# Gate products at eviction, short products queued later, and a pace of modulation loads by layer, in a four-layer RWKV-7 / GLA / SSD kernel

## The chip, the core and the metric

One of the eight cores of a Trainium2 chip runs the whole program; the seven others are idle. The metric is the device time of one execution in microseconds (us), the median of several runs. TensorE (PE) multiplies, VectorE (DVE) and ScalarE (ACT) work elementwise, SyncE (SP) and GpSimd (POOL) issue the transfers here.

## The reference, cut to what matters

A stream x of 256 tokens and 2048 features goes through four layers: RWKV-7, GLA, SSD, RWKV-7. Each layer adds to x:

```
mod = silu(c) @ ada_w[i] + ada_b[i]                  # 2048 x 6144 weights for a single vector c
shift, scale, gate = split(mod, 3)
h   = rms_norm(x, norm_g[i]) * (1 + scale) + shift
x   = x + gate * mixer(h)                            # then a final rms_norm
GLA, per head (4; keys 256, values 512):
  o = causal(q k^T with decays) v + q state          # chunks of 64
  y = rms_norm(o) * head_g * silu(g);  mixer = y @ w_out          # q, k, v, g: h @ w_in
SSD, per group (8; 8 heads of 64, state 128):
  x, B, C = silu(conv4(h @ w_in)), z = h @ w_in;  dt = softplus(...)
  y = causal(C B^T * decay) (x dt) + C state + d x   # chunks of 128
  y = rms_norm(y * silu(z), per group) * norm_g;  mixer = y @ w_out
```

## The kernel before

**Projections.** `jobs` computes blocks of 256 output columns. For each 128 x 1024 piece of weights (512 KB) it issues a load on SP into one of six `raw` buffers (`load_w`), lets ACT round it to H (L338) and DVE subtract it to L (L340), three buffers each, and issues 24 matmuls (L393: four k-tiles, two column tiles, three products of the split). Then it calls `tick`. "A tick" is such a piece below. The result lies in an `acc` bank of PSUM (two of them) and an `evac` function takes it out.

**Modulation.** The vector-matrix product with `ada_w` isn't done on PE: `ada_third` loads 128 x 1024 pieces (512 KB each, into the same six `raw` buffers, on the same SP queue) and DVE multiplies and accumulates them (L304; the first of 16 by ACT). Layer 0's shift and scale come first; then there are 320 pieces, 32 for each third (shift, scale, gate) of a layer. `tick` advances a generator over them: after tick n it has advanced `interp(n, PACE)` pieces, at most two more at a time, and not at all while `hold` is set (from the last output block of a layer until the next layer's first block is done). `ada_need` pulls at once, whatever is missing, when a layer needs a third: shift and scale at its start, the gate at its first output block. Pieces that `ada_need` pulls aren't counted by the pace.

**Layers in ticks.** Layer 0: 8 ticks of v (24 earlier pieces of v don't tick), 32 of k, 32 of r, 32 of g, and the output projection in three parts of 16, 16 and 8 ticks (`o4`, `o3`, `o1` below), together 144. Layer 1 (GLA): 4 for the decays, 8 for each head's v, 4 for q, 4 for k, 8 for g, and 16 for the output projection of each pair of heads, together 132, up to tick 276. Layer 2 (SSD): 2 for dt, then for each of eight groups 4 for B and C, 8 for x, 8 for z, and 16 for the output projection of each pair of groups, together 226, up to tick 502. Layer 3: 168.

**The order of the work.** A planner orders each engine's instructions when the program is built: it takes, by a model of the chip, the instruction that comes earliest in the program among those that it holds ready. The program's order is thus a priority and not the order of issue; at run time each engine follows the planned order. In a GLA head the program's order is v, q, k, then the scores (L1167), transposes of k (L1183), values (L1190 to L1200), the head's rms (L1204 to L1209), transposes of O (L1212) with an ACT copy to `oT`, then the output projection of the previous pair (`due()`), then g, whose `evg` (L1217 to L1224) computes silu(g), multiplies by `oT` and splits the result into `ys`, the input of the output projection. In an SSD group: B and C with their convolution, scores and decays (L1311 to L1341), x with its convolution, transposes of x (L1348), state (L1356), values (L1366 to L1372), `due()`, z with `evz` (L1375 to L1388), the group's rms (L1393, `inv_rms`) and `ys` (L1397). The last pair's output projection follows the last z or g at once; it goes through eight blocks, each over all k-tiles of the pair, two ticks each. After the last layer's last block `norm` sums squares (L454, L471), takes an inverse root by twelve small DVE operations (L1041 to L1049), and spreads it with a matmul (L483) before the next layer's input can be made.

Of the kernel before, what the change touches and what calls it, by code (L numbers as in the profile page):

```python
# [129 lines left out]
class Kern:  # L130
    def __init__(self, ctx, tc, A, out, layers=(0, 1, 2, 3), final=True):
# [15 lines left out]
        self.hold = False  # L147
        self.par = self.const.tile([P, NPAR], F32, name="par")
# [267 lines left out]
    def outproj(self, wv, k0, ys, i, norm=None):  # L416
# [10 lines left out]
        for n0 in range(0, D, cols):  # L427
            def evac(j, ps, n0=n0):
# [10 lines left out]
            self.hold = bool(norm) and n0 == D - cols  # L439
            self.proj(wv, n0, cols, ys, evac, k0=k0)  # L440
# [33 lines left out]
    def inv_rms(self, ps, mul, eps, bank):  # L474

        nc = self.nc
        rs = self.rsqrt_tiny(ps[:, 0:2], mul, eps, self.nrm)
        dg = self.nrm.tile([P, T], F32, name="xm", bufs=2)
        for c in range(2):
            nc.vector.tensor_scalar(out=dg[:, c * P:(c + 1) * P], in0=self.c("ident"), scalar1=rs[:, c:c + 1],  # L480
                                    scalar2=None, op0=ALU.mult)
        ps = bank()
# [627 lines left out]
    def paired(self, n, part, wout, i):  # L1110

        ys, k0, due = [], 0, []
        for g in range(n):
            ys += part(g, lambda: due and due.pop()())
            if g % 2:
                due.append(lambda ys=ys, k0=k0, norm=self.b1 if g == n - 1 else None:
                           self.outproj(wout, k0, ys, i, norm))
                ys, k0 = [], k0 + 8
        due.pop()()

    def gla_head(self, h, hs, win, bc, due, vt):
# [33 lines left out]
        self.proj(win, 1024 + 256 * h, 256, hs, evk)  # L1155


        HS = (slice(0, 64), slice(64, 128))
        ps = self.b1()
        for s in range(2):  # L1160
            for bi in range(2):
                i = slice((2 * s + bi) * C, (2 * s + bi + 1) * C)
                for kk in range(2):
                    for bj in range(2):
                        j = slice((2 * s + bj) * C, (2 * s + bj + 1) * C)
                        l, r = (ke, qe) if bi == bj else (kn, qs)
# [12 lines left out]

        kt = gu.tile([P, 2, P], F32, name="kt")  # L1180
        ps = self.b1()
        for kk in range(2):
            nc.tensor.transpose(ps[:, kk * P:(kk + 1) * P], kn[:, kk, 0:P], self.c("ident"))  # L1183
        nc.scalar.copy(out=kt.rearrange("p a c -> p (a c)"), in_=ps[:, 0:T])

        O = gu.tile([P, 2, 512], F32, name="O", bufs=1)
        S = gu.tile([P, 2, 512], F32, name="S")
        for s in range(2):
            ps = self.b1()
            nc.tensor.matmul(ps, sT[:, s, :], vt[:, s, :], start=True, stop=s == 0)  # L1190
            if s:
                for kk in range(2):
                    nc.tensor.matmul(ps, qs[:, kk, P:], S[:, kk, :], start=False, stop=kk == 1)
            nc.scalar.copy(out=O[:, s, :], in_=ps)
            if not s:
                for kk in range(2):
                    ps = self.b1()
                    nc.tensor.matmul(ps, kt[:, kk, :], vt[:, 0, :], start=True, stop=True)
                    nc.scalar.copy(out=S[:, kk, :], in_=ps)

        var = gu.tile([P, 2], F32, name="var")
        for tt in range(2):
            sq = gu.tile([P, 512], F32, name="osq", bufs=1)
            nc.scalar.activation(sq, O[:, tt, :], AF.Square)  # L1204
            nc.vector.tensor_reduce(out=var[:, tt:tt + 1], in_=sq, op=ALU.add, axis=mybir.AxisListType.X)
# [266 lines left out]
```

## Time and profile before

| | |
|---|---|
| median of 3 runs | 2873.01 us (2872.56 to 2883.22) |
| profiled execution | 2887.0 us, of which the span is 2885.0 |
| PE busy | 2686.2 us, 93% |
| DVE busy | 2212.4 us, 77% |
| ACT busy | 1392.8 us, 48% |
| granted TensorE clock, mean | 0.952 |
| moved by DMA | 673.68 MB, 234 GB/s over the span |

The busy shares are means over stages with different limits. In the tables of stretches below each engine's busy time stands with its number of instructions in brackets; PEclk is the mean granted clock of TensorE in the stretch as a share of 2.4 GHz. For layer 0 the stretches shown are k, r, g, o3, and o1 with the boundary to GLA. A stretch begins and ends at the first projection matmul (L393) of a stage, found by counting these matmuls in order of time (24 to a tick).

### The profile page before, as it was taken

How to read it: one execution, taken by the hardware profiler on the slowest of the kernel's cores; microseconds unless marked ns; L12 is line 12 of the kernel's file. 1: busy time of each engine (PE TensorE's matmuls, PEld its weight loads, DVE VectorE, ACT ScalarE, POOL GpSimd, SP SyncE). 2: the span in 40 equal slices, each digit the busy share in tenths (PEclk: the TensorE clock that was granted, in tenths of full speed). 3: DMA queues.
4: the chain of work that ended last, by engine and by line, in shares of the span. 5: the costliest groups of instructions: out<-in, count | busy, mean ns of one | idle time of the engine just before them, and what ended most of it. 6: DMA issues, size and time to landing. Idle time of an engine off the chain costs nothing.

```text
span 2885.0 us, 64064 instructions
## 1 busy us (share of the span) xinstructions
PE 2686.2 (93%) x26098; PEld 2505.1 (87%) x26098; DVE 2212.4 (77%) x3918; ACT 1392.8 (48%) x2315; POOL 154.6 (5%) x298
## 2 busy tenths in 40 slices
PE   6899999999987899988998999999889999999997
PEld 4789889887877899987988999999879988988887
DVE  5778777877788888877898788887668897666666
ACT  3475655433335454434544454554457756453333
POOL 0011110101000000000000000000000111010100
PEclk8899999999998999999999999999989999999999
DMA  9866557977677888976784767776557665585543
GB/s 348 308 231 190 176 161 261 347 266 278 207 261 244 293 285 291 324 268 197 277 294 161 242 219 228 224 226 216 167 171 236 230 208 190 178 297 194 207 132 108
DMA packets 239126, 673.68 MB, mean 234 GB/s; under 512 B 72272, under 2 KB 78416, under 8 KB 235760
## 3 DMA queue, kind: packets, MB, share of 16 engines
q1 hardware_dynamic: 217904, 580.84, 60.2%
q0 software_dynamic: 20928, 88.75, 8.5%
q8 instruction: 205, 3.36, 0.5%
q14 instruction: 89, 0.73, 0.1%
HBM read 620.66 MB, written 48.82 MB: 232 GB/s over the span
## 4 chain that ended last, share of the span: by engine, by line
PE 66%; DVE 8%; DMA 8%; issue 3%; ACT 2%; SPq 1%; POOL 0%; DVEq 0%; ACTq 0%; POOLq 0%
PE acc L393 53%; DMA raw<-in_ada_w 3%; DVE L L340 2%; PE g L785 2%; DVE adaacc L304 1%; ACT H L338 1%; PE b L897 1%; DMA raw<-in_gla_w_in 1%; DMA dx<-bd 1%; DMA raw<-in_rwkv_w_in 1%; PE b L866 1%; DMA raw<-in_rwkv_w_out 1%; PE b L873 1%; DMA sp<-yd 1%; PE b L1030 1%
## 5 line engine op out<-in xcount | busy, mean ns | idle before, releaser
L393 PE MATMUL acc<-xs,H 128*128 128x256 f32 x8480 | 1634.4, 291 | 36.5 <-ACT H L338 8.1
L393 PEld LDWEIGHTS acc<-xs,H 128*128 128x128 f32 x8480 | 1362.8, 196 | 69.3 <-ACT H L338 11.4
L393 PE MATMUL acc<-xs,L 128*128 128x256 f32 x4240 | 1230.6, 291 | 17.1 <-DVE L L340 16.2
L338 ACT CAST H<-raw 128x1024 fp32r<-128x1024 f32 (+1 forms) x706 | 718.0, 1018 | 854.9 <-PE acc L393 634.3
L340 DVE TENSOR_TENSOR L<-raw,H 128x1024 fp32r<-128x1024 f32 (+1 forms) x706 | 833.7, 1183 | 248.9 <-ACT H L338 234.0
L393 PEld LDWEIGHTS acc<-xs,L 128*128 128x128 f32 x4240 | 830.8, 196 | 31.1 <-DVE L L340 21.5
L304 DVE SCALAR_TENSOR_TENSOR adaacc<-raw,cact,adaacc 128x1024 f32<-128x1024 f32 x300 | 384.0, 1280 | 132.6 <-DMA raw<-in_ada_w 130.2
L393 PE MATMUL acc<-ys,H 128*128 128x256 f32 x1536 | 293.3, 291 | 12.2 <-DVE ys L409 4.9
L393 PEld LDWEIGHTS acc<-ys,H 128*128 128x128 f32 x1536 | 245.9, 195 | 22.0 <-issue 6.6
L393 PE MATMUL acc<-ys,L 128*128 128x256 f32 x768 | 222.1, 290 | 0.4 <-DVE L L340 0.4
L393 PEld LDWEIGHTS acc<-ys,L 128*128 128x128 f32 x768 | 149.6, 195 | 4.6 <-issue 3.6
L551 ACT ACTIVATE hn<-x,mod,omu 128x256 f32<-128x256 f32 x192 | 113.4, 599 | 1.5 <-DVE x L542 1.2
L431 DVE SCALAR_TENSOR_TENSOR x<-acc,mod,x 128x256 f32<-128x256 f32 x192 | 83.6, 477 | 35.7 <-PE acc L393 35.3
L393 PE MATMUL acc<-H,xs 128*128 128x256 f32 x512 | 97.1, 290 | 1.6 <-ACT vt L1078 1.6
L554 DVE SCALAR_TENSOR_TENSOR xm<-x,par,hn 128x256 f32<-128x256 f32 x192 | 88.6, 476 | 1.4 <-ACT hn L551 0.3
L393 PEld LDWEIGHTS acc<-H,xs 128*128 128x128 f32 x512 | 82.4, 197 | 3.1 <-ACT vt L1078 1.8
L393 PE MATMUL acc<-L,xs 128*128 128x256 f32 x256 | 73.8, 289 | 0.0
L785 PE MATMUL g<-abkp 64*128 64x128 f32 x768 | 65.8, 293 | 4.0 <-DVE G L823 2.7
L408 ACT CAST xs<-xm 128x256 fp32r<-128x256 f32 x128 | 50.9, 400 | 35.4 <-DVE xm L554 33.0
L785 PEld LDWEIGHTS g<-abkp 64*128 64x128 f32 x768 | 52.2, 190 | 15.8 <-issue 8.8
L1284 DVE SCALAR_TENSOR_TENSOR cva<-cvp,hcw,cva 128x256 f32<-128x256 f32 x144 | 64.9, 476 | 0.0
L278 DVE SCALAR_TENSOR_TENSOR adaacc<-raw,cact,adaacc 128x512 f32<-128x512 f32 x56 | 41.9, 748 | 27.5 <-DMA raw<-in_ada_w 23.0
(358 smaller groups left out, 3063.0 us busy)
## 6 DMA issues: line engine op xcount, KB each, us to landing
raw<-in_ada_w SPq DMA_DIRECT2D x384, 512.0 KB, 4.8
raw<-in_rwkv_w_in SPq DMA_DIRECT2D x256, 512.0 KB, 4.7
raw<-in_ssd_w_in SPq DMA_DIRECT2D x128, 512.0 KB, 4.4
raw<-in_gla_w_in SPq DMA_DIRECT2D x96, 512.0 KB, 5.2
raw<-in_ssd_w_out SPq DMA_DIRECT2D x64, 512.0 KB, 4.2
raw<-in_rwkv_w_out SPq DMA_DIRECT2D x48, 512.0 KB, 4.2
abkp<-kd POOLq DMA_DIRECT2D x16, 1024.0 KB, 7.3
raw<-in_gla_w_out SPq DMA_DIRECT2D x32, 512.0 KB, 4.9
```

The costliest lines, as they stand in the source:

```text
L278: nc.vector.scalar_tensor_tensor(out=acc, in0=raw[:, u, :], scalar=self.cact[:, k:k + 1], in1=acc, op0=ALU.mult, op1=ALU.add)
L304: nc.vector.scalar_tensor_tensor(out=acc, in0=raw, scalar=self.cact[:, k:k + 1], in1=acc, op0=ALU.mult, op1=ALU.add)
L338: nc.scalar.copy(out=hi, in_=raw[:, a:a + n])
L340: nc.vector.tensor_tensor(out=lo, in0=raw[:, a:a + n], in1=hi, op=ALU.subtract)
L393: self.nc.tensor.matmul(ps, lhs, rhs, start=first and part == 0 and w is hi, stop=last and w is lo)
L408: nc.scalar.copy(out=t[:, 0, :], in_=src)
L431: nc.vector.scalar_tensor_tensor(out=self.x[:, t, 1:], in0=ps[:, u, :], scalar=gate[:, t:t + 1], in1=self.x[:, t, 1:], op0=ALU.mult, op1=A ...
L551: nc.scalar.activation(t1, x[:, k, 1:], AF.Identity, scale=self.omu[:, col:col + 1], bias=self.mods[(i, 0)][:, k:k + 1])
L554: done[k] = nc.vector.scalar_tensor_tensor(out=xm, in0=x[:, k, 0:T], scalar=self.p("rwkv_mu", col), in1=t1, op0=ALU.mult, op1=ALU.add)
L785: self.nc.tensor.matmul(ps[h][:, n * C:(n + 1) * C], s[r, q, c * C:(c + 1) * C], t[r, q, c * C:(c + 1) * C], start=True, stop=True)
L866: nc.tensor.matmul(ps[r, n * H:(n + 1) * H], G[h][:, q, r], tk[:, 2, q, HS[h]], start=not c, stop=not c or h == 1)
L1284: nc.vector.scalar_tensor_tensor(out=a, in0=src[:, k:k + T], scalar=w[k], in1=a, op0=ALU.mult, op1=ALU.add)
```

## The change

1. GLA: `scores`, `values` and `turned` (transposes and `ys`) become functions that `put_off` runs a number of ticks later: 1 and 3 ticks after k, 2 ticks after g. `evg` stores (tanh + 1) g in `oT`; `turned` multiplies the transposed O, straight from PSUM, by head_g and `oT` on DVE (the factor 0.5 moves to O's scaling). The ACT copies to `oT` (eight of 128 x 128 for each head) go.
2. SSD: likewise `scores` 3 ticks after B and C, `turned` 3 and `states` 5 ticks after x, `values` of each half of z 2 ticks after that half, `sums` 4 and `scaled` 6 ticks after z. `evz` stores (tanh + 1) z in `yv`; `values` multiplies it in. The three transposes and products of B share one bank.
3. Output projection of the last pair of GLA and SSD: the first four blocks are done together in four banks, so k-tiles 0 to 3 (the earlier head or group) of all four come before k-tiles 4 to 7. `ys` is looked up when a k-tile is reached, and what is still put off is run then.
4. `PACE` has new knots.

```diff
-PACE = ((0, 60, 78, 150, 319, 530, 660), (0, 0, 16, 96, 234, 292, 320))
+PACE = ((0, 57, 134, 272, 496, 620), (0, 36, 98, 194, 290, 320))
+LATE = 2
+    def pairs(self, bank, n):
+        return [bank().rearrange("p (j t) -> p j t", j=2) for _ in range(n)]
 # tick
+        self.run_later(self.tk)
+    def put_off(self, n, part):
+        self.later.append((self.tk + n, part))
+    def run_later(self, tk=math.inf):
+        while self.later and self.later[0][0] <= tk:
+            self.later.pop(0)[1]()
 # outproj
+        blocks = [(n0, cols, taker(n0), cols, False) for n0 in range(0, D, cols)]
+        if lead:
+            n = len(lead) + 2
+            self.jobs(wv, blocks[:n], ys, k0, banks=lead)
+            blocks = blocks[n:]
+        for block in blocks:
+            self.hold = bool(norm) and block is blocks[-1]
+            self.jobs(wv, [block], ys, k0)
 # paired
+        def out(g, ys):
+            def rows(k):
+                if k >= len(ys[k // 4]) + k // 4 * 4:
+                    self.run_later()
+                return ys[k // 4][k % 4]
+            last = g == n - 1
+            self.outproj(wout, 4 * g - 4, Lazy(8, rows), i, self.b1 if last else None,
+                         self.pairs(self.b1, 2) if last else ())
 # gla_head
-                nc.scalar.activation(oT[:, v, tt * P:(tt + 1) * P], ps[:, v * P:(v + 1) * P], AF.Copy,
-                                     scale=self.p("gla_head_g", v))
+        def turned():
+            for w in range(2):
+                ps = self.b1()
 ...
+                for u in range(2):
+                    v = 2 * w + u
+                    nc.vector.scalar_tensor_tensor(out=oT[:, v, :], in0=ps[:, u * T:(u + 1) * T],
+                                                   scalar=self.p("gla_head_g", v), in1=oT[:, v, :], op0=ALU.mult,
+                                                   op1=ALU.mult)
+                    ys.append(self.parts(oT[:, v, :], None, gu, "ys", bufs=12))
+        self.put_off(1, scores)
+        self.put_off(3, values)
 ...
-                nc.vector.scalar_tensor_tensor(out=th, in0=th, scalar=1.0, in1=g, op0=ALU.add, op1=ALU.mult)
-                nc.vector.scalar_tensor_tensor(out=th, in0=th, scalar=0.5, in1=oT[:, j + u, :], op0=ALU.mult, op1=ALU.mult)
-                ys.append(self.parts(th, None, gu, "ys", bufs=12))
+                nc.vector.scalar_tensor_tensor(out=oT[:, j + u, :], in0=th, scalar=1.0, in1=ps[:, u, :], op0=ALU.add,
+                                               op1=ALU.mult)
         due()
         self.proj(win, 4096 + 512 * h, 512, hs, evg)
+        self.put_off(LATE, turned)
 # ssd_group
+        self.put_off(3, scores)
 ...
+                nc.vector.scalar_tensor_tensor(out=yv[:, j + u, :], in0=th, scalar=1.0, in1=ps[:, u, :], op0=ALU.add,
+                                               op1=ALU.mult)
+        def values(vs):
 ...
+                nc.vector.scalar_tensor_tensor(out=y, in0=xT[:, v, :], scalar=self.p("ssd_d", 4 * g + v), in1=ps[:, 0:T],
+                                               op0=ALU.mult, op1=ALU.add)
+                nc.vector.scalar_tensor_tensor(out=yv[:, v, :], in0=yv[:, v, :], scalar=0.5, in1=y, op0=ALU.mult,
                                                op1=ALU.mult)
+        self.put_off(3, turned)
+        self.put_off(5, states)
         due()
+        for n in range(2):
+            self.proj(win, 512 * g + T * n, T, hs, lambda _, ps, n=n: evz(2 * n, ps))
+            self.put_off(2, lambda n=n: values((2 * n, 2 * n + 1)))
 ...
+        self.put_off(4, sums)
+        self.put_off(6, scaled)
```

## Rows read from the trace of the kernel before

**Rows 1.** The page, part 1: busy time of PE and PE's weight loads.

```profile
PE 2686.2 (93%) x26098; PEld 2505.1 (87%) x26098; DVE 2212.4 (77%) x3918; ACT 1392.8 (48%) x2315; POOL 154.6 (5%) x298
```

**Rows 2.** The chain that ended last, in order of time: start, us, what.

```profile
1582.87 68.46 PE acc L393 x569
```

**Rows 3.** Stretch (us, length), busy PE, PEld, DVE, ACT, POOL; PEclk, DMA, GB/s: layer 0.

```profile
206.50:356.20 149.70, 144.01 (x1607) 136.60 (x1605) 122.45 (x273) 95.51 (x191) 17.84 (x32) 0.94 0.59 186
356.20:502.70 146.50, 137.35 (x2063) 130.42 (x2062) 101.75 (x183) 78.80 (x145) 13.26 (x27) 0.95 0.65 209
502.70:698.70 196.00, 188.16 (x2041) 168.14 (x2040) 150.72 (x241) 71.27 (x114) 23.21 (x43) 0.97 0.84 294
...
795.30:845.10 49.80, 41.50 (x336) 38.70 (x335) 41.29 (x66) 15.79 (x22) 0.00 (x0) 0.97 0.75 253
845.10:889.80 44.70, 25.73 (x160) 17.65 (x158) 37.62 (x67) 16.87 (x34) 0.00 (x0) 0.80 0.84 280
```

**Rows 4.** The same stages of layer 3: k, g, o3, o1.

```profile
2249.10:2400.90 151.80, 141.97 (x1423) 133.85 (x1422) 128.45 (x271) 93.09 (x181) 15.77 (x28) 0.92 0.64 207
...
2544.70:2717.80 173.10, 172.68 (x2023) 156.94 (x2022) 108.59 (x195) 65.23 (x107) 22.15 (x41) 1.00 0.66 230
...
2815.50:2850.40 34.90, 34.90 (x294) 34.90 (x293) 25.54 (x50) 14.54 (x20) 0.00 (x0) 1.00 0.46 144
2850.40:2866.30 15.90, 15.90 (x118) 12.63 (x117) 10.52 (x23) 9.38 (x20) 0.00 (x0) 1.00 0.06 18
```

**Rows 5.** By stretch, modulation instructions alone (tile adaacc): layer 0's g, o3, o1.

```profile
502.70:698.70 196.00, 2.29 (x24) 0.47 (x24) 43.55 (x34) 3.47 (x3) 0.97 0.84 294
...
795.30:845.10 49.80, 0.64 (x8) 0.16 (x8) 18.30 (x15) 1.15 (x1) 0.97 0.75 253
845.10:889.80 44.70, 1.72 (x16) 0.39 (x16) 19.93 (x16) 2.30 (x2) 0.80 0.84 280
```

**Rows 6.** The page, part 5: the modulation's DVE operation; one from PSUM.

```profile
L304 DVE SCALAR_TENSOR_TENSOR adaacc<-raw,cact,adaacc 128x1024 f32<-128x1024 f32 x300 | 384.0, 1280 | 132.6 <-DMA raw<-in_ada_w 130.2
...
L431 DVE SCALAR_TENSOR_TENSOR x<-acc,mod,x 128x256 f32<-128x256 f32 x192 | 83.6, 477 | 35.7 <-PE acc L393 35.3
```

**Rows 7.** DVE's timeline at the boundary of layers 0 and 1.

```profile
873.25 1.28 DVE L304 SCALAR_TENSOR_TENSOR adaacc<-raw,cact,adaacc 128x1024 f32<-128x1024 f32 x1
874.45 0.16 DVE L1042 TENSOR_SCALAR rst<-rsv 128x2 int32<-128x2 int32 x1
```

**Rows 8.** PE's waits from 870 to 890: total, times, longest.

```profile
PE mx L310 <- DVE rsr L1049: 10.0, 1, 10.0
```

**Rows 9.** By stretch: GLA's start, its last output; SSD's first three groups, last five, end.

```profile
889.80:992.10 102.30, 95.08 (x699) 87.96 (x700) 87.86 (x118) 57.98 (x87) 0.52 (x1) 0.94 0.71 246
...
1277.80:1358.80 81.00, 63.68 (x444) 54.64 (x442) 56.28 (x89) 29.92 (x53) 0.00 (x0) 0.86 0.69 231
1358.80:1640.10 281.30, 261.15 (x2101) 252.41 (x2102) 235.89 (x421) 138.04 (x201) 3.25 (x6) 0.94 0.70 238
1640.10:2057.30 417.20, 416.83 (x3551) 407.97 (x3550) 346.23 (x622) 212.75 (x303) 1.59 (x3) 1.00 0.69 223
2057.30:2135.80 78.50, 62.85 (x430) 54.04 (x428) 42.39 (x83) 28.57 (x48) 5.77 (x8) 0.89 0.47 154
```

**Rows 10.** PE's waits from 1277 to 1291, the end of GLA's last head.

```profile
PE b L1212 <- DVE O L1209: 3.3, 1, 3.3
PE acc L393 <- ACT ys L408: 2.3, 1, 2.3
PE acc L393 <- DVE ys L409: 1.6, 1, 1.6
```

**Rows 11.** By stretch: SSD's group 1, group 3, group 4 with an output projection.

```profile
1437.80:1512.20 74.40, 68.13 (x562) 65.86 (x562) 67.86 (x121) 37.21 (x56) 0.53 (x1) 0.95 0.85 295
...
1640.10:1706.10 66.00, 66.00 (x564) 63.62 (x563) 56.48 (x113) 35.66 (x53) 0.53 (x1) 1.00 0.63 209
1706.10:1816.10 110.00, 110.00 (x935) 108.71 (x934) 90.90 (x154) 53.49 (x74) 0.53 (x1) 1.00 0.73 235
```

More of the change, by code (lines that the diff above doesn't have):

```diff
@@ L147, in __init__ @@
         self.hold = False
+        self.later = []
         self.par = self.const.tile([P, NPAR], F32, name="par")
@@ L425, in outproj, with taker, evac @@
         cols = 2 * P
-        for n0 in range(0, D, cols):
-            def evac(j, ps, n0=n0):
+        def taker(n0):
+            def evac(j, ps):
                 for u in range(ps.shape[1]):
@@ L1110, in paired @@
     def paired(self, n, part, wout, i):
-        ys, k0, due = [], 0, []
+        due = []
+        def out(g, ys):
[6 more added lines that the diff above has]
+                         self.pairs(self.b1, 2) if last else ())
         for g in range(n):
-            ys += part(g, lambda: due and due.pop()())
+            new = part(g, lambda: due and due.pop()())
             if g % 2:
-                due.append(lambda ys=ys, k0=k0, norm=self.b1 if g == n - 1 else None:
-                           self.outproj(wout, k0, ys, i, norm))
-                ys, k0 = [], k0 + 8
+                due.append(lambda g=g, ys=(old, new): out(g, ys))
+            old = new
         due.pop()()
@@ L1189, in gla_head, with scores @@
+        def scores():
+            HS = (slice(0, 64), slice(64, 128))
             ps = self.b1()
[L1190 to L1199, printed above, removed]
@@ L1216, in gla_head @@
-        ys = []
+            for s in range(2):
+                for bi in range(2):
+                    i = slice((2 * s + bi) * C, (2 * s + bi + 1) * C)
+                    for kk in range(2):
+                        for bj in range(2):
+                            j = slice((2 * s + bj) * C, (2 * s + bj + 1) * C)
+                            l, r = (ke, qe) if bi == bj else (kn, qs)
+                            nc.tensor.matmul(ps[HS[bj], s * P + bi * C:s * P + (bi + 1) * C], l[:, kk, j], r[:, kk, i],
+                                             start=(kk == 0), stop=(kk == 1))
@@ L1287, in conv, with conv_evac, ev @@
         nc.vector.scalar_tensor_tensor(out=dst, in0=th, scalar=1.0, in1=a, op0=ALU.add, op1=ALU.mult)
+    def conv_evac(self, t0, dst, step=1):
+        nc = self.nc
+        def ev(j, ps):
+            cp = self.su.tile([P, 2, T + 3], F32, name="cvp")
+            nc.vector.memset(cp[:, :, 0:3], 0.0)
+            nc.scalar.copy(out=cp[:, :, 3:], in_=ps)
+            for u in range(2):
+                self.conv(t0 + j + u * step, cp[:, u, :], dst[:, j + u, :])
+        return ev
     def ssd_group(self, g, hs, win, acd, tk, due):
@@ new lines, in ssd_group, with turned @@
+        self.put_off(3, scores)
+        xT = su.tile([P, 4, T], F32, name="xT")
+        self.proj(win, 4096 + 512 * g, 512, hs, self.conv_evac(4 * g, xT))
+        xc = [su.tile([P, 8, 64], F32, name=f"xc{c}") for c in range(2)]
+        xd = su.tile([P, 8, 64], F32, name="xd", bufs=1)
+        def turned():
+            for c in range(2):
+                ps = self.b1()
+                for v in range(4):
+                    nc.tensor.transpose(ps[:, v * P:(v + 1) * P], xT[:, v, c * C:(c + 1) * C], self.c("ident"))
+                nc.vector.tensor_tensor(out=xc[c], in0=ps.rearrange("p (h d) -> p h d", d=64),
+                                        in1=tk[:, c, HG].unsqueeze(2).broadcast_to([P, 8, 64]), op=ALU.mult)
+            nc.vector.tensor_tensor(out=xd, in0=xc[0], in1=de.unsqueeze(2).broadcast_to([P, 8, 64]), op=ALU.mult)
```

211 lines of the change are left out of this document (96 added, 115 removed).

## The prediction, written before the changed kernel was built

> **What bounds the kernel now.** I read the page first: PE is busy 93% and its weight loads 87% of the span [rows 1], so at most some 200 us of PE idle time are to be had. Then the chain of waits, for the price of a tick: 569 projection matmuls in 68.46 us are 0.120 us each, 24 of them 2.89 us [rows 2]. Then I cut the span at the stages' first projection matmuls and took busy times by stretch, because the same stages occur twice. k, r and g are 768 matmuls each, 92.4 us of projection; the rest is RWKV's own work. Layer 0's k and layer 3's take 149.7 and 151.8 us; but g takes 196.0 against 173.1, o3 49.8 against 34.9, and o1 with the boundary 44.7, against 15.9 for o1 alone in layer 3 [rows 3, 4]. What differs is modulation: 37 pieces in layer 0's g (34 on DVE and 3 on ACT), 16 in o3, 18 at o1 [rows 5], each 1.28 us of DVE [rows 6] and 512 KB of DMA. DMA there is at 0.75 to 0.84 with DVE at 37.62 of 44.7 us [rows 3]. In SSD the last five groups run without a gap (PE 416.83 of 417.2) [rows 9], while dt and the first three take 281.3 us [rows 9], where two ticks of dt (5.8), two steady groups (66.0) and one with output (110.0) [rows 11] would take 248: 33 us are lost there. GLA loses at its start (PE 95.08 of 102.3, clock 0.94) and at its end (63.68 of 81.0, clock 0.86) [rows 9]. So PE's work is the floor; waits of a few us and pieces that come in bursts lie on top.
>
> **The pace, in ticks.** Old: after tick 40 no piece, after 72 10, after 104 44, after 136 80, after 143 88. Layer 1 needs 96 at tick 144, so `ada_need` pulls 8 at once, and after `hold` the pace catches up at two a tick: 31 pieces in the 16 ticks of GLA's first head (from 88 to 119). New: 5 pieces in v, 20 in k (old 0), 23 in r (old 10), 26 in g (old 34), 13 in each 16 ticks of output (old 18), 104 after tick 143, so nothing is pulled at layer 1, and 20 pieces in the first head. SSD: old 0.82 a tick until 319, then 0.275; new 0.43 throughout. Its gate needs 224 at tick 330, where the new pace stands at 218: 6 pieces are pulled there, which the old pace (237) didn't do. Layer 3's gate needs 320 at tick 630: old 313, new 320; 7 pulls go.
>
> **Costs, part by part** (us; minus is a gain; bounds in brackets).
> - *v, k and r of layer 0* get 5, 20 and 13 pieces more. The 20 are 25.6 us of DVE, beside 122.45 in a stage of 149.7 [rows 3, 6]: 148 in all, a full engine. Hidden, they cost 0; uncovered, 25.6. Nearest is layer 3's k: DVE 128.45, 151.8 us [rows 4], so part of it shows: +8. r has room (101.75 of 146.5): +2 (0 to +13, or 10 x 1.28); v +2 (0 to +6). SP also issues RWKV's small transfers, which queue behind loads that wait for a `raw` buffer; that is inside these bounds. Together +12 (0 to +45).
> - *g:* 22.9 us more than layer 3 for 37 pieces is 0.6 a piece; 11 fewer (26) give -7; a burst costs more at its top: -10 (-23 to 0).
> - *o3:* 14.9 us for 16 pieces; 3 to 5 go: -5 (-15 to 0).
> - *o1 and boundary:* 18 pieces become about 5. Thirteen are 16.6 us of DVE, and 6.8 MB, 24 us at the 280 GB/s there [rows 3, 6]. One wait shows it: PE waits 10.0 us [rows 8] while the twelve small operations of the inverse root stand on DVE between MACs of 1.28 [rows 7]. The chain without them remains: -14 (-24 to 0).
> - *GLA's start:* PE idle 7.2 us; 11 pieces fewer: -5 (-9 to 0). Scores and values are late in the program now; the planner put them among projections before, so I count them nothing here (-2 to +2).
> - *GLA's last output:* PE waits 3.3, 2.3 and 1.6 us at its start [rows 10], then runs at a lower clock (0.86 in the stretch). With four blocks on k-tiles 0 to 3, `turned` has 2 ticks ahead and 2 behind it, 5.8 us, for 4 products from PSUM and 4 subtractions on DVE, under 4 us if each takes the 0.48 us of an operation of that size [rows 6]. The oT copies off ACT are hidden work. -11 (-17, all idle time, to 0).
> - *SSD's first three groups:* 33 us over the steady ones, of which DMA and DVE (67.86 of 74.4) [rows 11] are the cause as much as the short products. The pieces in groups 0 and 1 fall from 32 to 18. The 6 pulled at tick 330 are 3.1 MB, 10.7 us at 295 GB/s, against three buffered ticks, 8.7: some 3 us, up to 8 if DVE is behind. Net -18 (-33 to +8).
> - *SSD's last five groups:* 37 pieces become 58: 27 us of DVE on 346.23 of 417.2, then 89%. No gap is there to win: +4 (0 to +27). `evz` and `values` keep three DVE operations for each 128 columns.
> - *SSD's last output:* sums come 4 ticks after z, at the very end of the four blocks' first half; the rms chain behind them stays bare, only a wait in front of it goes, of 15.7 us without PE work in that stretch (62.85 of 78.5) [rows 9]: -3 (-8 to +2).
> - *Layer 3:* PE had no gap where 7 pulls go: 0 (-5 to +5).
> Sum: 12 - 10 - 5 - 14 - 5 - 11 - 18 + 4 - 3 = -50. The profiled execution took 2887.0 us (span 2885.0, 2.0 around it), 14 above the median 2873.01; as profiled the sum gives 2837, against the median 2823, which I forecast.
>
> **A rule weighed.** k's DVE would stand at 148 of 149.7 us [rows 3]. The Trainium skill (Perfetto Trace Analysis, Identifying the Most-Contended Engine) takes Vector's occupancy as a fair measure of its closeness to its limit. By it the stage still just fits and the extra pieces in v, k and r cost about 1 instead of 12, total 2812; no row here shows a stage at such a share. A second: it gives 358 GB/s as a core's share of HBM (DMA: Bandwidth & Descriptors, Specifications). By that the 13 pieces at o1 are worth 19 us rather than 24 at most; the rows at that place stay at 280.
>
> **Rivals.**
> A. *The planner had it already.* Later queueing only changes priorities, and the planner already mixed short products with projections: five SSD groups show no gap. Then parts 1 to 3 give nothing and the pace alone acts: GLA's end 0, SSD's end 0, SSD's start half: -50 + 11 + 3 + 9 = -27, 2846. Against: the three waits at GLA's end are behind the last projection, where the planner has nothing to put.
> B. *The bytes stay.* The same 384 pieces pass through the same DMA and DVE; spread, they give back later what they gave: g and o3 0, SSD's start -5, GLA's start 0, the rest as forecast: +12 - 14 - 11 - 5 + 4 - 3 = -17, 2856. Rounded for the pull at 330 it is within the bound of no change. For: DVE waits 130.2 us for these loads in all [rows 6], so it isn't full everywhere; against: PE's idle time sits in bursts.
> C. *DVE becomes the bound, slower.* Where pieces are added they cost their full 1.28 us (v, k and r +45, SSD's last groups +27) and the pull at tick 330 costs 8 + 3: +83. Gains elsewhere, SSD's first part without the pull -21: -10 - 5 - 14 - 5 - 11 - 21 - 3 = -69. Net +14, 2887. It decides once more than 83% of the added price shows. For: k at 82% already; against: layer 3's k has 6.0 us more DVE work than layer 0's and takes 2.1 us longer [rows 3, 4].
> D. *All waits go:* half of the way from each forecast to its lower bound, about -50 - 40 = -90, 2783. The lower bounds are sums of idle time that another wait can take up, so I hold it unlikely.
>
> **Chances.** Forecast 0.55 (2823, itself 2800 to 2845), A 0.17, B 0.11, C 0.08, D 0.09. Range for 8 in 10: 2788 to 2866, reaching over A and B and most of the way to D. A measurement here can tell about 0.5%, 14 us: faster is below 2858.6, slower above 2887.4. The forecast, A, D and a little of B make faster 0.83; the rest of B and half of C same 0.11; half of C slower 0.06.
>
> **What would show it.** Right: layer 0's g falls to about 185, o1 with the boundary to about 31, no MAC between the operations of the inverse root there; the three waits at GLA's end gone and its last stretch near 70; dt and SSD's first three groups near 263. Wrong: layer 0's k over 165 with DVE above 95%, or PE gaps on L (L340) in SSD's last five groups (over 425 us); a new PE gap about 2 ticks behind the third group's x, where 6 pieces are pulled. I am wrong in kind if the pace's stages stay as they are and the gain is in the queueing, and wrong altogether if the early stages of layer 0 lose more than 45.

## The result, and the profile after

The changed kernel takes 2906.3 us (median of 4 runs, 2894.2 to 2909.4); beside it the kernel before takes 2873.2. The ratio is 1.0089, interval 1.0065 to 1.0113 (the two medians alone would give 1.0115): slower by about 0.9%, where 2823 was forecast. The profiled execution took 2909.4 us (span 2907.3, 22.3 above the span before). The profile before is of an execution 14 us above its median, so the stages below show less of the loss than the medians do.

Page of the changed kernel, parts 1, 4 and 5 (answers to [rows 1, 6]):

```profile
PE 2691.8 (93%) x26098; PEld 2505.4 (86%) x26098; DVE 2209.5 (76%) x3918; ACT 1387.2 (48%) x2283; POOL 154.4 (5%) x298
...
PE 59%; DMA 17%; DVE 17%; issue 5%; ACT 2%; SPq 1%; DVEq 0%; POOL 0%; ACTq 0%; POOLq 0%
...
L309 DVE SCALAR_TENSOR_TENSOR adaacc<-raw,cact,adaacc 128x1024 f32<-128x1024 f32 x300 | 384.4, 1281 | 247.3 <-DMA raw<-in_ada_w 245.8
```

DVE does no more work than before, but it stands 245.8 us in front of modulation loads, against 130.2 [rows 6]. Its share of the chain is 17%, 8% before; DMA's is also 17%, 8% before.

Stretches of the changed kernel, columns as in [rows 3]: layer 0's k, r, g, first output blocks (o4), o3, o1; GLA's start and last output; dt to SSD's group 2; groups 3 to 7; SSD's end (answers to [rows 3, 9]); then group 1 and group 2 alone.

```profile
211.50:361.70 150.20, 138.63 (x1435) 129.89 (x1434) 131.65 (x256) 90.63 (x175) 14.67 (x28) 0.97 0.76 251
361.70:517.10 155.40, 147.29 (x2038) 138.16 (x2037) 126.04 (x235) 87.60 (x164) 15.78 (x31) 0.90 0.70 236
517.10:691.40 174.30, 161.43 (x1835) 147.44 (x1833) 125.32 (x192) 64.54 (x101) 19.40 (x36) 0.96 0.83 300
691.40:807.70 116.30, 108.97 (x1264) 95.62 (x1265) 87.69 (x176) 33.73 (x58) 11.36 (x22) 0.98 0.58 193
807.70:856.00 48.30, 44.94 (x419) 42.57 (x417) 36.88 (x64) 18.77 (x29) 1.07 (x2) 0.96 0.71 234
856.00:886.40 30.40, 19.39 (x136) 14.04 (x135) 23.54 (x54) 13.50 (x29) 0.00 (x0) 0.94 0.59 180
886.40:985.30 98.90, 94.10 (x699) 87.96 (x700) 84.21 (x114) 58.38 (x87) 0.52 (x1) 0.93 0.72 243
1274.00:1341.50 67.50, 60.23 (x444) 51.62 (x443) 48.60 (x80) 28.03 (x45) 0.00 (x0) 0.96 0.68 213
1341.50:1618.60 277.10, 256.82 (x2079) 247.31 (x2080) 226.26 (x397) 134.60 (x197) 2.72 (x5) 0.96 0.67 231
1618.60:2077.90 459.30, 432.96 (x3554) 418.80 (x3552) 370.61 (x657) 218.12 (x309) 2.12 (x4) 0.97 0.69 227
2077.90:2158.20 80.30, 65.21 (x462) 55.23 (x460) 45.63 (x90) 27.82 (x47) 5.77 (x8) 0.88 0.48 164
...
1413.30:1478.90 65.60, 65.60 (x564) 63.46 (x563) 60.94 (x118) 36.46 (x56) 0.53 (x1) 1.00 0.71 238
1478.90:1618.60 139.70, 121.69 (x975) 116.02 (x974) 102.27 (x166) 55.03 (x75) 0.53 (x1) 0.94 0.66 227
```

In these two profiles the whole loss is in SSD's groups 3 to 7: 459.3 against 417.2 us. Layer 0's o1 fell as forecast (30.4). g fell from 196.0 to 174.3, but o4 behind it rose. The kernel before, o4 and all of k to o1:

```profile
206.50:889.80 683.30, 625.53 (x7120) 571.51 (x7118) 526.94 (x967) 306.14 (x550) 62.88 (x118) 0.94 0.72 240
698.70:795.30 96.60, 88.79 (x926) 79.99 (x923) 73.11 (x140) 27.89 (x47) 8.57 (x16) 0.93 0.69 233
```

o4 has 1264 matmuls now, 926 before, and g 1835, 2041 before: the planner moved short work across the cut. From k to o1 the gain is 8.4 us (674.9 against 683.3), in all of layer 0 3.7.

In SSD's group 2, at tick 330, where `ada_need` pulls 6 pieces, PE waits (total, times, longest), and DVE's timeline shows why:

```profile
PE b L516 <- DVE xm L509: 10.5, 1, 10.5
```

```profile
1528.96 1.28 DVE L309 SCALAR_TENSOR_TENSOR adaacc<-raw,cact,adaacc 128x1024 f32<-128x1024 f32 x1
...
1531.30 0.15 DVE L1081 SCALAR_TENSOR_TENSOR rst<-rst,rsv 128x2 f32<-128x2 f32 x1
...
1535.18 1.28 DVE L309 SCALAR_TENSOR_TENSOR adaacc<-raw,cact,adaacc 128x1024 f32<-128x1024 f32 x1 [0.94 <-DMA raw<-in_ada_w]
...
1537.84 0.48 DVE L509 TENSOR_SCALAR xm<-cst,rsr 128x128 f32<-128x128 f32 x2
```

The multiply-adds (MACs) stand between the steps of the inverse root, as they did at layer 1's boundary before [rows 7, 8], with the convolution's steps and subtractions beside them: the burst was moved, not removed. The kernels of experiment 1 have the same wait in group 2 with the new pace (10.3 and 9.3 us in e2 and e3), and at most 3.1 us with the old one (e1).

### The profile page after: what moved, and what is told of

Its sections match the earlier page's. It is cut to its first block, busy times and chain, and to the rows that moved or that the text cites. A ratio compares the mean times of both kernels' runs of the same rounds, so it can differ in the third digit from the quotient of the medians.

```text
span 2907.3 us, 63994 instructions
## 1 busy us (share of the span) xinstructions
PE 2691.8 (93%) x26098; PEld 2505.4 (86%) x26098; DVE 2209.5 (76%) x3918; ACT 1387.2 (48%) x2283; POOL 154.4 (5%) x298
## 4 chain that ended last, share of the span: by engine, by line
PE 59%; DMA 17%; DVE 17%; issue 5%; ACT 2%; SPq 1%; DVEq 0%; POOL 0%; ACTq 0%; POOLq 0%
PE acc L402 45%; DMA raw<-in_ada_w 11%; DVE L L345 5%; DVE adaacc L309 2%; PE pv L402 2%; PE g L818 2%; DMA raw<-in_rwkv_w_in 1%; DMA dx<-bd 1%; PE b L402 1%; PE b L930 1%; ACT H L343 1%; DMA xd<-dx 1%; DMA bd<-LT 1%; DVE M L1384 1%; PE b L899 1%
## 5 line engine op out<-in xcount | busy, mean ns | idle before, releaser
L309 DVE SCALAR_TENSOR_TENSOR adaacc<-raw,cact,adaacc 128x1024 f32<-128x1024 f32 x300 | 384.4, 1281 | 247.3 <-DMA raw<-in_ada_w 245.8
L402 PE MATMUL acc<-ys,H 128*128 128x256 f32 x1408 | 267.7, 289 | 5.8 <-DVE ys L427 4.8
L402 PEld LDWEIGHTS acc<-ys,H 128*128 128x128 f32 x1408 | 223.6, 193 | 16.9 <-issue 8.8
L402 PE MATMUL acc<-ys,L 128*128 128x256 f32 x704 | 203.1, 289 | 6.0 <-DVE L L345 5.7
L402 PEld LDWEIGHTS acc<-ys,L 128*128 128x128 f32 x704 | 135.5, 193 | 10.4 <-DVE L L345 6.6
L818 PEld LDWEIGHTS g<-abkp 64*128 64x128 f32 x768 | 50.3, 187 | 14.7 <-issue 7.4
```

The source lines that it names most:

```text
L309: nc.vector.scalar_tensor_tensor(out=acc, in0=raw, scalar=self.cact[:, k:k + 1], in1=acc, op0=ALU.mult, op1=ALU.add)
L818: self.nc.tensor.matmul(ps[h][:, n * C:(n + 1) * C], s[r, q, c * C:(c + 1) * C], t[r, q, c * C:(c + 1) * C], start=True, stop=True)
```

## The experiments

Each ratio is to the kernel before on the same chip, with its 95% interval. "SSD" below is the stretch of groups 2 to 7, 545.1 us before, 599.0 after; "pieces" are those whose MACs (DVE's and ACT's) run in it, 46 before and 78 after. Times of stages are from one profile each, cut as ahead of the prediction.

**1. Which part costs: four recombinations.**

```
e1_oldpace, on the changed kernel:
- PACE = ((0, 57, 134, 272, 496, 620), (0, 36, 98, 194, 290, 320))
+ PACE = ((0, 60, 78, 150, 319, 530, 660), (0, 0, 16, 96, 234, 292, 320))
e2_pace_only, on the kernel before: the same with - and + exchanged
e3_no_ssd, on the changed kernel:    - its ssd_group    + ssd_group of before
e4_gla_lead: e3 with e1's PACE (so GLA's put_off calls and lead blocks alone)
```

> The changed kernel with the old pace knots; all of the later queueing stays. SSD from group 2 to group 7 took 545 us before and 599 after, and that is where the time went. Theory pace (more modulation pieces in SSD's later groups, each MAC waiting for its own load in DVE's order, stretch the group's rms chain until PE waits): that stretch falls back to 545 to 555, DVE's wait for modulation loads to about 130 us in all, and the total to 2865 to 2880, since the pace's gain at the first boundary and SSD's start goes too. Theory queue (the put-off products crowd DVE work into the ticks of B, C and x): the stretch stays at 590 to 600, total 2910 to 2925.

> The kernel before with the new pace knots alone. Theory pace: SSD's groups 2 to 7 take 590 to 600 us here too, DVE's wait for modulation loads is about 245 us, total 2910 to 2920 (the after kernel without GLA's 13 us). Theory queue: the stretch stays near 545, the gains at the first boundary and SSD's start remain, total 2845 to 2858.

> The changed kernel with SSD's group as before (nothing put off in SSD); new pace, GLA's queueing and the four blocks at once stay. Theory pace: SSD's groups 2 to 7 stay at 590 to 600, total 2900 to 2912. Theory queue: the stretch falls to 545 to 550, total 2845 to 2860.

> The kernel before with GLA's queueing and the four blocks at once; old pace, SSD's group as before. Both theories: GLA's last output 12 to 14 us shorter and the rest as before, 2858 to 2864. If it stands at 2873 or above, the planner's redrawn order moves single stages by ten us whatever is changed, and differences of that size between these kernels say little.

| | us | ratio | SSD us / pieces | layer 0 | GLA |
|---|---|---|---|---|---|
| before | 2873 | 1 | 545.1 / 46 | 848.5 | 469.0 |
| after | 2906 | 1.0089 | 599.0 / 78 | 844.8 | 455.1 |
| e1 | 2888 | 1.0023 (1.0002 to 1.0044) | 558.1 / 46 | 847.1 | 462.2 |
| e2 | 2919 | 1.0142 (1.0112 to 1.0172) | 584.8 / 78 | 846.5 | 465.1 |
| e3 | 2908 | 1.0099 (1.0069 to 1.0130) | 587.4 / 79 | 845.9 | 457.5 |
| e4 | 2865 | 0.9957 (0.9936 to 0.9979) | 547.0 / 46 | 833.8 | 458.0 |

The pace alone costs 1.42% on the kernel before (e2), and about as much with GLA's part (e3 against e4). In SSD that is 39.7 us for 32 more pieces, 1.24 each: a MAC's whole 1.28. Layer 0 has 8 pieces more and gains nothing or a little. GLA's parts gain 0.4%; its last output takes 73.1 us in e4 against 81.0, 8 us less and not the 12 to 14 expected. The changed SSD group costs 13 us of its own in SSD (e1 against before). In the totals the pace costs less on top of it (after against e1, 0.66%), though in SSD it costs the same there, 40.9 us; one profile each can't say why.

**2. Is it DVE's work or its wait for the load?** All three kernels are e2 with the MACs of the thirds that run in SSD and layer 3 altered. e5b and e6 leave out most of what these MACs compute; f1 computes the same on POOL.

```
e5b_resident  - in0=raw          + in0=ident (resident), loads stay
e6_short_mac  - acc, raw         + acc[:, 0:8], raw[:, 0:8]
f1_pool       - vector MAC       + gpsimd.tensor_scalar (raw*cact), gpsimd.tensor_tensor (acc+raw)
```

> The kernel before with the new pace alone, and one thing more: the modulation's multiply-adds that run in SSD and in layer 3 (thirds (2,2), (3,0), (3,1), (3,2)) read a resident constant instead of the loaded piece; the loads stay, so bytes, queue and DVE's instruction count are unchanged, and only the wait of DVE for the load is gone. What they compute is left out. Theory 'wait' (DVE runs in program order and each added multiply-add holds the short SSD work behind it until its own load lands): SSD groups 2 to 7 fall from 585 us back to 545 to 555, total 2875 to 2885. Theory 'work' (DVE and DMA are simply full where the pieces fall): groups 2 to 7 stay at 575 to 590, total 2905 to 2918.

> The kernel before with the new pace alone; the same multiply-adds (thirds (2,2), (3,0), (3,1), (3,2)) still wait for their loads but work on 8 of their 1024 columns, so some 1.2 us of DVE's work goes with each and the wait stays. What they compute is left out for the other columns. Theory 'wait': SSD groups 2 to 7 stay at 570 to 588 us, total 2900 to 2918. Theory 'work': they fall to 545 to 555 us, total 2875 to 2885, and DVE's idle time before these operations grows while PE's does not.

> The kernel before with the new pace alone (2919 us), and the multiply-adds of thirds (2,2), (3,0), (3,1), (3,2) (120, of which 78 run in SSD groups 2 to 7) moved from DVE to POOL, as a product and a sum there. Nothing is left out; loads, bytes and buffers stay, only DVE's 1.28 us a piece and its wait go. Theory 'DVE in program order is the bound of SSD' (both its work and its wait): groups 2 to 7 fall from 585 us to 535-555 and the total to 2845-2880, as with the short multiply-adds (534 us, 2843). Theory 'the loads and the buffers are the bound' (a piece holds one of six buffers and DMA time, whoever reads it): groups 2 to 7 stay at 570 or more, total over 2900, the more so if POOL holds a buffer longer than DVE's 1.28 us.

SSD in the kernel before, in e2, e5b, e6 and f1:

```profile
1512.20:2057.30 545.10, 536.26 (x4532) 523.75 (x4533) 444.18 (x803) 268.40 (x380) 2.65 (x5) 0.99 0.67 217
```

```profile
1497.80:2082.60 584.80, 544.08 (x4508) 526.41 (x4507) 473.13 (x822) 272.33 (x381) 2.64 (x5) 0.98 0.69 231
```

```profile
1493.70:2049.70 556.00, 537.47 (x4495) 524.86 (x4495) 473.97 (x820) 269.52 (x380) 2.65 (x5) 0.98 0.69 239
```

```profile
1479.90:2014.30 534.40, 530.61 (x4509) 519.51 (x4508) 400.98 (x807) 267.47 (x381) 2.11 (x4) 1.00 0.75 252
```

```profile
1512.80:2138.60 625.80, 562.24 (x4508) 542.01 (x4507) 563.95 (x743) 270.31 (x382) 450.63 (x151) 0.94 0.63 216
```

DVE's waits there, before, in e2 and in e6:

```profile
DVE adaacc L304 <- DMA raw<-in_ada_w: 40.9, 31, 3.5
DVE L L340 <- ACT H L338: 35.2, 38, 1.7
```

```profile
DVE adaacc L304 <- DMA raw<-in_ada_w: 87.7, 48, 5.0
DVE L L340 <- ACT H L338: 8.3, 12, 1.7
```

```profile
DVE adaacc L305 <- DMA raw<-in_ada_w: 64.0, 41, 3.5
DVE L L341 <- ACT H L339: 47.7, 50, 1.7
```

Both theories were half right. Without the wait (e5b, 2901 us, 1.0094, 1.0058 to 1.0130) SSD returns to 556, though layer 3 takes 16 us more than before. With the wait but without the work (e6, 2843 us, 0.9882, 0.9854 to 0.9909) it falls to 534, under the kernel before. The wait of 10.3 us in group 2 is gone in both. So both count on one in-order engine: busy plus waiting for loads is 485 of 545 us before (89%), 561 of 585 in e2 (96%), 570 of 599 after (95%, of which 96.7 us are the wait), 465 of 534 in e6 (87%). The second row is the reserve: DVE waiting for fresh H means that it has caught up with the weights. It was 35.2 us, and in e2 only 8.3 are left.

The sum isn't the whole account. e5b has 474 of 556 us (85%) and 53.2 us of reserve, and still stands 11 us above the kernel before; PE waits there for z's eviction:

```profile
PE acc L396 <- DVE cvt L1383: 13.6, 3, 6.7
```

e5b also frees each buffer when its load has landed, and e6 1.06 us sooner, which isn't separated here. But late weights don't hold SSD up: in e2 ACT waits only 7.6 us for weight loads in all of it.

f1 missed what the first theory said and fell where the second had put it: 2997 us, 1.0414 (1.0390 to 1.0438), SSD 625.8. The trace shows another cause than late loads: ACT waits 15.7 us for weights, but DVE, with no MACs left, was busy 564 us, against 379 in e2 without its MACs (the last section says why). POOL's product and sum take 3.6 and 2.6 us. f5_half_pool, the same for half of the pieces from GLA on, on top of e4:

> The kernel before with GLA's queueing and leading output blocks (2865 us, old pace), and the second half of each third from (1,2) on (16 pieces of 32, run in GLA, SSD and layer 3) computed on POOL as a product and a sum instead of DVE's multiply-add. If DVE in program order still bounds GLA's and SSD's first groups at the old pace: GLA and SSD's groups 0 to 2 gain 15 to 30 us, total 2835 to 2850. If at the old pace DVE has room there: 2860 to 2870. If POOL's two passes hold a buffer long enough to delay projection weights: slower, over 2875, with PE gaps on H or L.

It took 3065 us, 1.0644 (1.0617 to 1.0672); GLA alone 578 instead of 458. That is where its third theory had put it: in GLA, ACT waits 227 us for weight loads (26 in e4), and PE 37.8 us for L and 34.6 for H.

**3. What the changed SSD group costs.** All on e1; each tries one reason why the rows for the output come late.

```
e7_rms_early    - put_off(4, sums), put_off(6, scaled)     + put_off(2, ...) for both
f6_values_now   - put_off(2, values), 4, 6                 + put_off(0 if n else 2, values), 2, 4
g1_decay_early  decay's subtractions and exponentials out of scores(), at the group's start
h1_products_first
  - y = d*xT + ps; yv = 0.5*yv*y           (values, 2 ticks behind z)
  + xT = d*xT + ps                         (put_off(4, ...) behind x, ahead of z)
  + yv = 0.5*yv*xT                         (behind z)
  - put_off: turned 3, states 5, sums 4, scaled 6     + 2, 3, 2, 4
```

> The changed kernel with the old pace, and in SSD the sums of squares and the scaled rows put off by 2 ticks instead of 4 and 6. The changed SSD group lost 13 us in groups 2 to 7 (558 against 545), nearly all of it 9 to 10 in each group that carries output blocks after it. If the later inverse-root chain does that (its DVE steps fall among the output blocks' subtractions): groups 2 to 7 return to about 547 and the total falls from 2887 to 2868-2876. If it is something else in the group (the gate product at eviction, the short products' place): they stay at 555 to 562, total 2884 to 2893.

> The changed kernel with the old pace (2888 us), and in SSD the short products of the last two z blocks queued at once instead of two ticks later, the sums of squares 2 and the scaled rows 4 ticks behind instead of 4 and 6. In the changed group the inverse root's first DVE step comes 22 us after the next group's first projection, in the group before 13, and the scaled rows 49 against 36, with the output blocks due at 49: if that lateness is SSD's 13 us, groups 2 to 7 return from 558 to 545-550 and the total to 2870-2880. If the gate product at eviction or the scores' place does it: 556 to 562, total 2880 to 2892.

> The changed kernel with the old pace (2888 us), and in its SSD group the decay matrices' 16 subtractions and two exponentials, which need no projection, placed at the group's start instead of inside the put-off scores. In the group before, their exponentials ended up ahead of the group's first projection (2.6 us ahead), in the changed one 12 us behind it, and the inverse root's first step came at 21 to 22 us instead of 12.5 to 14.4, the last scaled subtraction at 52 instead of 40, where the output waits for it. If that displaced work is what makes it late: groups 2 to 7 return from 558 to 545-550 us and the total to 2870-2880. If not: 555 to 560 and 2882 to 2892.

> The changed kernel with the old pace (2888 us), and in its SSD group the short products taken ahead of z's projection (4 ticks behind x, their results stored over x), while z's gate product stays at its eviction and one multiplication joins them behind it. If the single buffer of the decay matrices is the cause (their last reader moved behind z, so the next group's decay work starts 12 to 15 us later and stands inside the inverse root): the exponentials return to about the next group's first projection, the root's first step from 21-22 to 12-16 us, the last scaled subtraction from 52 to about 40, groups 2 to 7 from 558 to 543-550 us, total 2868 to 2880. If the gate's place is the cause: the exponentials return, but groups 2 to 7 stay at 555 to 560 and the total at 2882 to 2892.

| | us | ratio | SSD us |
|---|---|---|---|
| e1 | 2888 | 1.0023 (1.0002 to 1.0044) | 558.1 |
| e7 | 2882 | 1.0009 (0.9991 to 1.0027) | 559.7 |
| f6 | 2889 | 1.0032 (1.0011 to 1.0053) | 554.6 |
| g1 | 2883 | 1.0014 (0.9994 to 1.0034) | 559.3 |
| h1 | 2867 | 0.9966 (0.9944 to 0.9988) | 538.9 |

The first three missed; h1 shows the cause. Group 4 with its output in e1 and in h1 (first matmul at 1685.0 and 1688.1):

```profile
1685.00:1804.80 119.80, 115.00 (x944) 112.34 (x943) 91.40 (x155) 53.14 (x72) 0.53 (x1) 0.97 0.63 209
```

```profile
1688.10:1798.50 110.40, 110.27 (x935) 108.78 (x934) 89.76 (x153) 53.45 (x74) 0.53 (x1) 1.00 0.71 232
```

In e1, the last product that reads M (PE) and the first subtraction into M of the next group (DVE); then the decay's exponentials (ACT), the root's first step and the last subtractions of the output's rows (DVE), and PE's wait; then the same from the exponentials on in h1:

```profile
1692.58 0.39 PE L1432 MATMUL b<-M,xc 128*64 128x128 f32 x4
...
1694.11 1.26 DVE L1384 TENSOR_SCALAR M<-ab,dtk 128x128 f32<-128x128 f32 x6
...
1697.12 2.00 ACT L1387 ACTIVATE M<-M 128x1024 f32<-128x1024 f32 x2
...
1706.34 0.15 DVE L1074 TENSOR_SCALAR rsv<-b 128x2 f32<-128x2 f32 x1
...
1736.49 1.09 DVE L427 TENSOR_TENSOR ys<-yv,ys 128x256 fp32r<-128x256 f32 x3
```

```profile
PE acc L402 <- DVE ys L427: 3.9, 2, 3.6
```

```profile
1685.32 1.04 ACT L1387 ACTIVATE M<-M 128x1024 f32<-128x1024 f32 x1
1687.20 1.06 ACT L1387 ACTIVATE M<-M 128x1024 f32<-128x1024 f32 x1
...
1700.48 0.16 DVE L1074 TENSOR_SCALAR rsv<-b 128x2 f32<-128x2 f32 x1 [1.39 <-PE b L1458]
...
1728.59 0.42 DVE L427 TENSOR_TENSOR ys<-yv,ys 128x256 fp32r<-128x256 f32 x1
```

Against the group's first matmul the exponentials stand at +12.1 in e1 and at -2.8 and -0.9 in h1, the root at +21.3 and +12.4, the last line of subtractions at +51.5 and +40.5. M (`M0`, `M1`) has one buffer; its last reader is the products, and the change put them behind z. In e1 they end at +8.0 and the next group's subtractions into M start at +9.1; in g1, which puts these subtractions first in the group, they still start at +9.1; in f6, with the last products queued two ticks earlier, at +7.4; in h1 at -5.5. So the next group's decay work starts late and falls among the root's steps. Program order could hardly mend it (e7, f6, g1): a buffer held it. h1 also takes the transposes and states earlier, which no run tests alone; f6 has its times for the root and the rows and gained only 3.5 us. Of the 9.4 us, 4.8 are PE's idle time; the rest goes with a granted clock of 0.97 instead of 1.00 (115.00 us busy for 944 matmuls against 110.27 for 935).

**4. Where pieces are cheap: the pace by place.** e8, f3 and g4 are e4 with another PACE, g3 is the changed kernel with f3's, g2 is g1 with it, h2 is h1 with it.

```
- PACE = ((0, 60, 78, 150, 319, 530, 660), (0, 0, 16, 96, 234, 292, 320))
+ PACE = ((0, 48, 143, 319, 530, 660), (0, 0, 97, 234, 292, 320))               e8_layer0_pace
+ PACE = ((0, 60, 78, 150, 272, 530, 660), (0, 0, 16, 96, 232, 292, 320))       f3_pace_gla
+ PACE = ((0, 60, 78, 150, 272, 530, 660), (0, 0, 16, 96, 256, 300, 320))       g4_more_gla
```

> The kernel before with the GLA queueing and the four leading output blocks (2865 us), and of the pace only its part up to the first boundary made even: a piece count of 97 at tick 143 instead of 88 plus a pull of 8, SSD's and layer 3's pace as before. If the pull at the boundary cost what the prediction said: layer 0's o1 with the boundary falls from 43 to about 31 us and the total to about 2855. If DMA and DVE give it back in the stages before: k, r, g and o3 together lose as much, total 2862 to 2868. SSD groups 2 to 7 stay at 545 to 550 either way.

> The kernel before with GLA's queueing and leading output blocks (2865 us), and of the pace only the middle moved the other way: 232 pieces by tick 272 (old 196), then 292 at 530 as before, so GLA has some 150 pieces instead of 116, SSD's groups 0 and 1 about 10 instead of 31, groups 2 to 7 as before. If a piece is cheap in GLA (21 fewer there gave 4 us) and 0.5 us in SSD's groups 0 and 1: GLA +7 to +10, dt to group 1 from 146 to about 137, group 2 with output from 128 to 115, total 2845 to 2858. If GLA's DVE has no room (58.96 of 65.7 us busy in its first head, 67.16 of 78.3 in its second): GLA +25 to +45, total 2868 to 2890.

> The kernel before with GLA's queueing and leading blocks, and 24 more pieces again in GLA (256 by tick 272, about 170 in GLA instead of 146), 15 fewer in SSD. SSD's groups 3 to 7 stand at PE's own time already (no PE gap), so they can give nothing more; if GLA is near DVE's limit, each added piece costs 0.5 to 1.28 us there: GLA 485 to 505 us, total 2865 to 2885. If GLA still has room: 473 to 480, total 2848 to 2858.

> The changed kernel with only its pace replaced by the one that puts 36 more pieces into GLA and has SSD's groups 2 to 7 at some 39 pieces instead of 78. If the place of the pieces is the cause of the loss: from 2906 down to 2865-2880, and layer 0 and layer 3 as they were within 10 us. If the rest of the change costs it: over 2890.

> The kernel of the run above with the pace that puts 36 more pieces into GLA (232 by tick 272). If the decay's place cures the changed group and the pace's gain adds to it: 2845 to 2862, groups 2 to 7 at 528 to 535. If the changed group stays late: 2862 to 2878, each group with output near 118.

> The run above with the pace that puts 36 more pieces into GLA. If both act: groups 2 to 7 at 526 to 532 us as with the group before (529), total 2845 to 2860. If the changed group stays late: 550 to 556, total 2863 to 2872, as measured with the pace alone (2868).

| | us | ratio | layer 0 | GLA us / pieces | dt to group 1 | SSD us / pieces |
|---|---|---|---|---|---|---|
| e4 | 2865 | 0.9957 | 833.8 | 458.0 / 116 | 145.7 / 31 | 547.0 / 46 |
| e8 | 2877 | 0.9983 (0.9964 to 1.0003) | 851.8 | 456.4 / 109 | 153.0 / 29 | 546.5 / 46 |
| f3 | 2854 | 0.9929 (0.9903 to 0.9956) | 842.5 | 473.3 / 146 | 138.2 / 10 | 528.8 / 39 |
| g4 | 2881 | 1.0009 (0.9987 to 1.0030) | 848.8 | 502.4 / 170 | 141.9 / 6 | 524.9 / 29 |
| g3 | 2868 | 0.9951 (0.9932 to 0.9969) | 845.0 | 475.2 / 146 | 136.6 / 9 | 553.2 / 40 |
| h2 | 2858 | 0.9939 (0.9917 to 0.9961) | 840.5 | 474.3 / 146 | 134.8 / 10 | 530.4 / 39 |

e8 took o1 with the boundary from 43.4 to 31.0 us, as the prediction's step said, but layer 0 as a whole (851.8) is no shorter than in the other kernels with the old pace (833.8 in e4 to 851.5 in h1): r, o4 and o3 gave it back, and its total is above both of its ranges. Of the kernels that leave nothing out f3 is the fastest, with h2 level. Thirty more pieces in GLA cost 15 us (0.5 each), the next 24 cost 29 (1.2 each): GLA has a knee too. GLA from its start in f3 and in g4:

```profile
883.70:1357.00 473.30, 444.51 (x3498) 413.70 (x3498) 406.32 (x528) 211.42 (x291) 0.52 (x1) 0.97 0.86 308
```

```profile
890.00:1392.50 502.50, 455.63 (x3511) 416.37 (x3511) 434.58 (x553) 212.82 (x293) 0.52 (x1) 0.97 0.88 315
```

ACT's waits for GLA's own weights there, in e4, f3 and g4:

```profile
ACT H L343 <- DMA raw<-in_gla_w_in: 25.6, 15, 4.5
```

```profile
ACT H L343 <- DMA raw<-in_gla_w_in: 93.6, 49, 4.8
```

```profile
ACT H L343 <- DMA raw<-in_gla_w_in: 130.2, 56, 4.8
```

Here the weights themselves come late, while DVE's busy time and its waits for modulation loads stay at 88% of GLA in f3 and in g4, with 31.1 and 37.5 us of reserve. So the knee is not SSD's. That leans to the loads, but no run holds DVE (86% busy in both) or DMA (0.86 and 0.88) fixed. g3 is the changed kernel with nothing but its pace replaced: 38 us faster. g2_all_best (g1's decay with f3's pace) took 2867 us, as g3, with SSD 553.5: late as in g1.

## Why the prediction was wrong

Profiled terms, forecast against measured. Layer 0 from v on: -17, measured -3.7. GLA's start -5, -3.4; its last output -11, -13.5; the rest of GLA 0, +3.0. dt to group 2: -18, -4.2. Groups 3 to 7: +4, +42.1. SSD's end -3, +1.8. Layer 3 0, -0.1. They sum to +22.0, the spans differ by 22.3.

- **The step that failed is "SSD's last five groups: 37 pieces become 58: 27 us of DVE on 346.23 of 417.2, then 89%. No gap is there to win: +4 (0 to +27)".** The pieces came as counted (57). But it took DVE's busy share as its load and left out the wait for loads in program order. With that wait DVE stood at 89% in groups 2 to 7 already and went to 95%. Of the 42.1, 23.7 come with the pace (e2's groups 3 to 7 take 440.9), 20.1 with the changed group (e1's 437.3), and with the products ahead of z nothing of that is left (h1's 417.6). The second had no place in the sum: I read the moved products as a change of priority and didn't ask which buffer they hold.
- **The pull at tick 330** was seen and priced at 3, up to 8; the pieces it pulls are behind one wait of 10.5, beside other waits. dt to group 1 gained 16 us, and group 2 took 11.8 back. The -4.2 is two changes: the new pace alone has +7.6 from dt to group 2 (e2), the rest of the change with the old pace -12.5 (e1), so the pace took back most of that gain.
- **Layer 0's terms** failed as a sum. One profile can't show it, since the same layer 0 takes 833.8 to 851.5 us in the 13 profiles with the old knots there (mean 844.2); the six with the new ones have 843.4, so the forecast -17 is about -1. By these means v to r lose 14.7 (forecast 12), o1 gains 14.4 (14), and g's 20.1 come back as 20.9 in o4, which the sum left at nothing: a stage that ends sooner is no gain where the planner carries short work over the cut. Pieces moved inside layer 0 are nearly free both ways (e8, e2).
- **GLA's queueing and lead blocks** gained, but less than the -11 forecast. The -13.5 at the last output is two changes: e4, with the old pace, has -8.0 there; e2, with the new pace alone, -3.8. The changed kernel has 10 pieces in that stretch instead of 17. That the number came out near the forecast is in part luck.
- **GLA's start** gave -3.4, but not for the reason forecast: the old pace reaches 119 only at tick 179, not within the first head's 16 ticks, and the stretch went from 26 pieces to 22, not from 31 to 20.
- **Rival B** (0.11) had layer 0 about right (-2 by its terms): the pieces spread there gave back later what they gave.
- **Rival C** had the mechanism (DVE the bound, the full price) and 0.08. It held in SSD, at 97% of the MAC's time a piece, and not in layer 0, where it put most of its loss.
- **The rule weighed.** k's DVE stood at 131.65 of 150.2 us, not at 148, and k lost nothing at its cut. But v, k and r together took 475.5 us against 461.4, near the 12 forecast and not the 1 by the rule. And the Trainium skill (Perfetto Trace Analysis, Identifying the Most-Contended Engine) would have group 2, with Vector busy 102.27 of 139.7 us (73%), further from its limit than group 1 with 60.94 of 65.6 (93%). Group 1 has no PE gap and group 2 waits for DVE. The measurement decides: for an in-order engine that waits for loads, occupancy isn't closeness to the limit. With its waits for loads (31.6 and 3.6 us) group 2 stands at 96% and group 1 at 98%: both are near it, and only the waits in PE's rows tell which loses.

## What to carry to other kernels

Before adding work to an in-order engine, add its waits at the head of its queue to its busy time, and look for its reserve (here DVE's wait for H): in SSD, where it was nearly gone, each added operation cost its full time. Neither is a rule by itself: e5b lost 11 us with room left on DVE, and in GLA a piece cost 1.2 us with reserve left, where the weights came late. When operations move later, ask which single buffer their operands hold and who fills it next; three changes of priority left most of that loss, and freeing the buffer earlier removed it. And compare stages by sums over several, since a planner moves work across any cut.

## What the runs showed of the hardware

Beside work on POOL most of DVE's operations took longer. The same operations in SSD on DVE, in e2 and in f1 (line, shape, count, then busy us and mean ns of one):

```profile
L340 DVE TENSOR_TENSOR L<-raw,H 128x1024 fp32r<-128x1024 f32 x169 | 204.9, 1219 | 9.2 <-ACT H L338 8.3
L1284 DVE SCALAR_TENSOR_TENSOR cva<-cvp,hcw,cva 128x256 f32<-128x256 f32 x108 | 49.0, 478 | 0.0
L431 DVE SCALAR_TENSOR_TENSOR x<-acc,mod,x 128x256 f32<-128x256 f32 x48 | 20.9, 478 | 8.4 <-PE acc L393 8.2
```

```profile
L345 DVE TENSOR_TENSOR L<-raw,H 128x1024 fp32r<-128x1024 f32 x169 | 257.7, 1531 | 43.0 <-ACT H L343 42.0
L1289 DVE SCALAR_TENSOR_TENSOR cva<-cvp,hcw,cva 128x256 f32<-128x256 f32 x108 | 83.5, 810 | 0.7 <-ACT cva L1287 0.7
L436 DVE SCALAR_TENSOR_TENSOR x<-acc,mod,x 128x256 f32<-128x256 f32 x48 | 20.8, 474 | 7.4 <-PE acc L398 7.4
```

The subtraction went from 1219 to 1531 ns and the convolution's step from 478 to 810, while the eviction that reads one input from PSUM stayed at 474. The Trainium skill (SBUF — State Buffer, Who interferes with whom) says that a Vector operation with two SBUF inputs contends with GpSimd's SBUF reads; the traces agree. The decay's subtraction into M, with a single tensor as input, went from 280 to 578 ns too, which that sentence doesn't cover. None of the theories ahead of f1 had this in it: POOL, busy 5% before, was no free room.
